# A two-layer hybrid attention kernel: the scores' product with the keys' low part on 128 rows

## The chip, the cores and the metric

The kernel runs on one core of one Trainium2 chip. The metric is the time of one execution on the device in microseconds (us); the kernel before takes 2376.73 us, the median of three runs (2375.67 to 2378.95). The rows below are from one more execution, taken by the hardware profiler. PE is TensorE's matmul, PEld its weight load, DVE is VectorE, ACT is ScalarE, POOL is GpSimd and SP is SyncE.

## The reference

Two layers work on 512 tokens of a sequence and 256 of a context, width 2048, all in float32. Layer 0 mixes pooling with latent attention of 12 heads; layer 1 mixes a matrix memory with attention of 16 heads in windows. Around both stand norms with an adaptive modulation, projections and a gate. Cut to the two attentions:

```python
def block_dense_attention(q, k, v):          # layer 0: head width 128 + 64 (rotated part)
    s = jnp.einsum('bqhd,bkhd->bhqk', qi, k).astype(F32) * scale
    p = jax.nn.softmax(s, axis=-1).astype(v.dtype)
    return jnp.einsum('bhqk,bkhd->bqhd', p, v)
...
def window_attention(q, k, v, kc, vc, sink): # layer 1: head width 64
    s_loc = jnp.einsum('bnqhgd,bnkhd->bnhgqk', qb, kb).astype(F32) * scale
    s_loc = jnp.where(mask[None, :, None, None], s_loc, -jnp.inf)
    s_ctx = jnp.einsum('bnqhgd,bchd->bnhgqc', qb, kc).astype(F32) * scale
    p = jax.nn.softmax(jnp.concatenate([s_loc, s_ctx, s_sink], axis=-1), axis=-1)
    ...
```

The rotated part of a latent head's keys is one vector of 64 numbers per token, shared by all 12 heads. In the window attention 8 query heads share one of two key heads of width 64. The sequence's queries see up to three blocks of 128 local keys and all 256 keys of the context.

## The kernel before

Every float32 operand of a matmul is held as two parts, a high part (rounded to the type float32r) and a low part, the rest. A product of two such operands is made of three: high by high, high by low, low by high. `split` (L108, L109) makes the parts: ACT copies the high part, DVE subtracts.

**A packed query.** Where the contraction is only 64 wide, the kernel puts both parts of a query into one tile of 128 rows: one half of the partitions holds the high part, the other half the low part (`qs` in the latent attention, L661 to 667; `wq` in the window attention, L1406 and L1407). Which half holds the high part depends on the head's parity. The keys stand twice, once on each half: KH and KL for the latent attention's rotated part (L432, L433, L480), KHw and KLw for the window attention (L1538 to L1552). One product of a packed query with KH gives high by high plus low by high. The third product, high by low, takes the half `hs` of the query's tile that holds the high part, and the same half of KL: 64 rows instead of 128.

**Latent attention** (650 to 1040 us). A unit is 256 queries of one head; there are 12 heads with three units each, and the third is the context's, which sees 256 keys instead of 768. `s_stage` (L669 to L693) computes the scores of 128 queries into a PSUM tile s: five products (three for the 128 wide part, then KH, then KL), each once over 512 keys and once over 256, or once over 256 alone in the third unit. DVE takes the maximum (L690), ACT the exponential (L691), DVE scales (L693). `t_stage` transposes the probabilities on PE (L708) and splits them, `o_stage` multiplies them with the values (L726). Between these parts PE works on the projections of later heads (L619, L639) and, for the last heads, on the out-projection (L776): `run(n)` issues a set number of columns of them. PE's order is the order of the program text (`manual_schedule`); the order on DVE and ACT is found by a scheduler, with `high_priority` for the softmax and the splits.

**Window attention** (1915 to 2245 us). `Softmax.heads` (L1452 and after) computes the scores of two heads for 128 queries. For each of the two heads it issues the KHw products with the local keys (L1461) and the context's (L1462). Then come the KLw products (L1466), for the local keys of the first and the second head, then for the context's keys of the first and the second head; the two heads of a pair use opposite halves of the partitions. There are 32 such calls; the outer two blocks of queries see 256 local keys, the inner two 384. DVE adds the mask and takes the maximum (L1470, shown as ISA or CUSTOM_DVE). `w_values` transposes a block of 128 keys' probabilities into wpt (L1583), splits it into wph and wpl, and multiplies with the values (L1593, L1594). In between, `run` issues products of the next projections and of the out-projection (L1419).

Of the kernel before, what the change touches and what calls it, by code (L numbers as in the profile page):

```python
# [9 lines left out]
F32R = mybir.dt.float32r  # L10
# [6 lines left out]
P = 128  # L17
# [11 lines left out]
# columns of the packed vector table  # L29
V_GB, V_SINK, V_PS, V_QN, V_KVN, V_HN, V_FN, V_NW, V_AB = 0, 16, 32, 36, 40, 44, 52, 68, 132  # L30
V_N = 132 + 192
# columns of the constant matrices
# [6 lines left out]
def tile_hybrid_dit(ctx: ExitStack, tc: tile.TileContext, ts: dict, out: bass.AP, dbg=None, upto=99):  # L39
# [6 lines left out]
    class Banks:  # L46
        """a PSUM pool: how many buffers each tag has; the buffers of pm can be taken out of their turn"""
# [16 lines left out]
    class Ring:  # L64
        """the buffers of one tag of a pool"""
# [45 lines left out]
    def load_w(src, n=1024, w=256, low=V):  # L111
        """-> for each block of 128 rows its (high, low) parts [128, w]"""
        raw = wp.tile([P, 1024], F32, name="wraw", tag="wraw", bufs=3)
        DM.dma_start(raw[:, :n], src)
        res = []
        m = n // 2
        for i in range(2):
            wh = wp.tile([P, 512], F32R, name="wh", tag="wh", bufs=4)
            wl = wp.tile([P, 512], F32R, name="wl", tag="wl", bufs=4)
            split(raw[:, i * m : (i + 1) * m], wh[:, :m], wl[:, :m], low)  # L120
            res += [(wh[:, k * w : (k + 1) * w], wl[:, k * w : (k + 1) * w]) for k in range(m // w)]
        return res

# [1 line left out]
    def ada_place(u, pb, n):  # L125
        """pb: [32, vectors, 16], column 32 b + c of the unit at [c, :, b]"""
# [7 lines left out]
    def ada_steps(u, pp, tp, nb=3, nt=2):  # L134
        """one unit of 512 columns on the tensor engine, in four steps"""
# [18 lines left out]
    def ada_vec_steps(u, pp, tp, nb, ttag, tbufs):  # L154
        """one unit of 512 columns on the vector engines: partial sums on every partition, then their sum"""
# [30 lines left out]
    class Background:  # L186
        """modulation units done step by step between other work; a unit's last product comes a few steps into the next one"""
# [30 lines left out]
    def rstd_col(ps6, nb, mul=None, bufs=2):  # L218
        """[128 tokens, nb] mean squares -> 1/rms"""
# [12 lines left out]
    def rows(v3, nb, pp, rb):  # L232
        """[128 tokens, nb] -> rb [128, nb*128], the same on every partition"""
# [24 lines left out]
    def h_chunk(j, xt, rb, u0, layer, hh, hl, tp, vs=(0, 1), low=V):  # L258
        """chunk j of the modulated rows; vs: 0 sequence, 1 context; rb, hh, hl: one AP for each"""
# [19 lines left out]
    def tmode(px, pc, w, kcs, Hx, Hc, first, last):  # L279
        """features on partitions; px/pc: one AP for each block of 128 columns; Hx/Hc: chunks (h, l)"""  # L280
# [12 lines left out]
    def kmode(ps, w, kcs, Hs, first, last, share):  # L293
        """tokens on partitions; ps: one AP for each block of 128 tokens; share: blocks in one bank"""
# [14 lines left out]
    def do_rope(ps, r, tmp):  # L309
        """ps [128, >=512] -> r[:, :512] rotated"""  # L310
# [11 lines left out]
    # =====================================================================  # L322
    # layer 0: pooling and latent attention
    # =====================================================================
    es0 = ExitStack()      # h
    esP = ExitStack()      # psum of the first phases
# [17 lines left out]
    # startup: statistics, modulation, h, and the first four blocks of columns  # L344
# [44 lines left out]
    def load_kr(q):  # L389
        """high and low parts of four chunks of the weights of k_r"""  # L390
# [6 lines left out]
    EARLY = 4           # units up to this one load beside the unused half of h  # L397
    PLAN = (0, 2, 3, 3, 2)      # blocks of columns done behind the steps of the next unit
# [43 lines left out]
    def c_evac(pairs, ssq):  # L442
        """raw latents and the sum of their squares"""
# [24 lines left out]
    # k_r of the context (its columns twice)  # L468
# [26 lines left out]
    # c_q  # L495
# [10 lines left out]
    # pooling  # L506
    m = NP - 16

    def pool_mean(g, px, pc):
        """difference between the windows' means and the values, split"""  # L510
# [57 lines left out]
    # a_gate  # L568
# [42 lines left out]
    # projections of the heads: generators that yield after every few products  # L611
# [57 lines left out]
    def s_stage(un, qi):  # L669
        """scores of 128 queries and their softmax"""  # L670
# [5 lines left out]
        hs = slice(64 * (head % 2), 64 * (head % 2) + 64)  # L676
        s = new_s2()
        qq = slice(u * 256 + qi * P, u * 256 + qi * P + P)
        prs = ((qh[:, qq], kh), (qh[:, qq], kl), (ql[:, qq], kh), (qs[:, qq], KH), (qs[hs, qq], KL[hs]))
# [68 lines left out]
    # the first group of the out-projection starts with the sequence's rows of the chunks that fit beside the last heads  # L748
# [3 lines left out]
    def zx_load(js):  # L752
        """sequence's part of two chunks"""
# [40 lines left out]
    def run(n):  # L794
        """n columns more"""
        state[0] += n
        while state[0] > 0:
            m = next(fill, None)
            if m is None:
                return  # L800
            state[0] -= m

    units = [(h, u) for h in range(12) for u in range(3)]
    FILL = ((3700, 4500, 4500), (3700, 4500, 4500), (2200, 2200, 2200))      # columns after each part of a unit
    SLOW = {(10, 0): 0.5, (10, 1): 0.5, (10, 2): 0.5, (11, 0): 0.3, (11, 1): 0.3, (11, 2): 1}      # what is left for the last two heads
    HEAD = 12 * NT      # columns of one projection of a head
# [59 lines left out]
    def zc_load(q):  # L866
        """context's part of four chunks"""
# [28 lines left out]
    def stats1(v):  # L896
        """1/rms of the sequence or of the context on every partition, in place of the sum"""
# [10 lines left out]
    # layer 1's rows of the sequence, while the context goes through  # L908
# [21 lines left out]
    # =====================================================================  # L930
    # layer 1: matrix memory and window attention
    # =====================================================================
# [31 lines left out]
    mm = opool(e2, "mm")          # what the matrix memory keeps  # L964
    C0 = [(mm.tile([P, 258], F32R, name=f"c0h{i}"), mm.tile([P, 258], F32R, name=f"c0l{i}")) for i in range(8)]
    emv = ExitStack()
    cm = opool(emv, "cmv")        # context only
    mkc = (cm.tile([P, 2, 512], F32R, name="mkch"), cm.tile([P, 2, 512], F32R, name="mkcl"))

    # v of head 0 with the gates  # L970
# [34 lines left out]
    # k  # L1005
# [13 lines left out]
    # gates  # L1019
# [16 lines left out]
    S.activation(g2, g1, AF.Exp, scale=-1.0)              # e = exp(-|f|)  # L1036
    V.tensor_scalar(g3, g2, 1.0, None, op0=ALU.add)       # y = 1 + e
    S.activation(g4, g3, AF.Ln)
    V.tensor_scalar(g1, g3, 1.0, None, op0=ALU.subtract)  # y - 1
    V.tensor_tensor(g1, g2, g1, op=ALU.subtract)          # what 1 + e lost  # L1040
    V.reciprocal(g2, g3)
    V.tensor_tensor(g1, g1, g2, op=ALU.mult)
    V.tensor_tensor(g4, g4, g1, op=ALU.add)               # log1p(e)
# [9 lines left out]
    # context: log weights of its positions in its final state  # L1053
    acol = gs.tile([P, 2, 2, 4], F32, name="acol")
    pa_ = pmt("pac", [P, 2, 2, 4])
    for d in range(2):
        far, near = (0, 1) if d == 0 else (1, 0)   # the far block also decays over the whole near one
# [27 lines left out]
    # sequence: local cumulative sums, block totals, running maxima  # L1085
# [18 lines left out]
    negM = [gp.tile([36, 4, P], F32R, name=f"negM{d}") for d in range(2)]   # high parts in rows 0-3, low ones in 32-35  # L1104
# [41 lines left out]
    # exp(-m_t), the inter-block offsets, the exponents' biases  # L1146
# [17 lines left out]
    # v of the other heads  # L1164
# [29 lines left out]
    # keys and values of the window attention  # L1194
# [178 lines left out]
    # first window group, while the last head goes through  # L1373
# [39 lines left out]
    def steps(px, w, kcs, bs, Hs, first, last):  # L1413
        """products of some chunks with some blocks of columns, one at a time"""
# [7 lines left out]
    def w_proj(i):  # L1422
        """queries and gates of a group"""
# [20 lines left out]
    class Softmax:  # L1444
        """scores of four heads for 128 queries and their softmax"""
# [6 lines left out]
        def heads(self, pair):  # L1452
# [7 lines left out]
            for a, s in zip(pair, ss_):  # L1460
                T.matmul(s[:, 512 - nl : 512], qs[i][a][:, qq], KHw[g][:, b0 * P : b1 * P], start=True, stop=False)  # L1461
                T.matmul(s[:, 512:768], qs[i][a][:, qq], KHw[g][:, NX:], start=True, stop=False)  # L1462
            for dst, ks in ((slice(512 - nl, 512), slice(b0 * P, b1 * P)), (slice(512, 768), slice(NX, NT))):
                for a, s in zip(pair, ss_):
                    hf = slice(64 * (a % 2), 64 * (a % 2) + 64)
                    T.matmul(s[:, dst], qs[i][a][hf, qq], KLw[g][hf, ks], start=False, stop=True)  # L1466
# [23 lines left out]
    def out_steps(g, px):  # L1490
        """all but the last two chunks"""
# [17 lines left out]
    def fillers():  # L1509
        """the other groups' projections, then the first three groups of the out-projection"""  # L1510
# [14 lines left out]
    PRE, PRE2, PRE3, RATE, RATE_END = 16, 8, 20, 9.5, 13      # products done ahead, and for each block of keys  # L1525
# [11 lines left out]
    # keys: rotated, split, each kv head on both halves of the partitions  # L1537
# [15 lines left out]
    vhl = ap2.tile([P, 6, 2, P], F32R, name="vhl")      # high and low parts side by side  # L1553
# [7 lines left out]
    # masks over the local blocks and the context  # L1561
# [12 lines left out]
    def w_values(i, nb, kc, prs, st_):  # L1574
        """one block of 128 keys: its part of what the four heads attend to, [features, queries] of their two blocks"""
# [259 lines left out]
```

## Time and profile before

| what | value |
|---|---|
| three timed runs, median (lowest, highest) | 2376.73 us (2375.67, 2378.95) |
| span of the profiled execution, first to last instruction | 2376.1 us |
[...]
| PE busy over the span | 2269.3 us |
| PEld busy | 1897.2 us |
| DVE busy | 1492.2 us |
| ACT busy | 1041.0 us |
| POOL busy | 462.4 us |

The profiled execution's own device time is not listed apart from its span; the median of the timed runs is 0.6 us above the span, which is what lies around the first and the last instruction. Busy time of PE is the union of its matmuls' durations. These overlap: the next matmul starts long before the one before it has ended, so the pace is read from the starts. A row of the timeline gives the start, the length, the engine, the line, the operation, what it writes and reads, the rows and columns of the array that it uses (128\*128, or 64\*128 for a product on half of the rows), its shape and how many like it follow one another directly; idle time of the engine just before it stands in brackets.

### The profile page before, as it was taken

The page shows a single profiled execution, that of the slowest core. Times are in us where ns is not written, and L with a number is a line of the kernel's source. Part 1 is how long each engine was busy: PE and PEld are TensorE (multiplying, and loading weights), DVE is VectorE, ACT ScalarE, POOL GpSimd, SP SyncE. Part 2 cuts the span into 40 slices and gives each one's busy share as a digit, 9 for nine tenths or more (in the row PEclk, how much of TensorE's full clock was granted, in tenths as well). Part 3 has the DMA queues.
Part 4 walks back from the last instruction along what each step waited for, and adds up shares of the span by engine and source line. Part 5 has one row for each costly group of instructions (what it writes and reads, how often), then busy time and mean ns, then how long its engine had stood idle before and what let it go on. Part 6 is the DMA issues. An engine that isn't in the chain of part 4 may idle for free.

```text
span 2376.1 us, 34745 instructions
## 1 busy us (share of the span) xinstructions
PE 2269.3 (96%) x12920; PEld 1897.2 (80%) x12920; DVE 1492.2 (63%) x2748; ACT 1041.0 (44%) x2054; POOL 462.4 (19%) x393
## 2 busy tenths in 40 slices
PE   5999998899999999999999999999999999998997
PEld 3678887788888888878888798998888877776886
DVE  5578888866466666668767822522555576778435
ACT  4234444443344444454224522222555556666333
POOL 0015575754100000016311200000000000003111
PEclk9999999999999999999999999999999999999998
DMA  9854454553211111255675322123222211113333
GB/s 384 312 195 160 169 186 155 186 200 137 81 47 58 47 52 54 70 169 206 227 246 190 136 100 80 56 79 112 98 97 96 102 58 65 60 63 116 133 120 138
DMA packets 118586, 311.27 MB, mean 131 GB/s; under 512 B 13676, under 2 KB 21356, under 8 KB 118416
## 3 DMA queue, kind: packets, MB, share of 16 engines
q1 hardware_dynamic: 111536, 281.73, 34.5%
q0 software_dynamic: 6880, 27.32, 3.0%
q8 instruction: 101, 1.65, 0.3%
q14 instruction: 69, 0.57, 0.1%
HBM read 279.37 MB, written 29.62 MB: 130 GB/s over the span
## 4 chain that ended last, share of the span: by engine, by line
PE 70%; DVE 8%; issue 3%; ACT 2%; DMA 2%; POOL 2%; SPq 0%; DVEq 0%; ACTq 0%; POOLq 0%
PE px L289 20%; PE px L302 11%; PE pj L619 6%; PE pc L291 5%; PE px L1419 5%; PE s L683 5%; PE pc L302 3%; PE om L726 3%; PE pj L639 2%; PE s L1419 2%; PE po L1338 2%; PE tp L708 2%; POOL acc L169 1%; DVE wl L109 1%; DMA at<-in_ada_dram 1%
## 5 line engine op out<-in xcount | busy, mean ns | idle before, releaser
L109 DVE TENSOR_TENSOR wl<-wraw,wh 128x512 fp32r<-128x512 f32 (+2 forms) x556 | 429.9, 780 | 422.9 <-ACT wh L108 414.8
L108 ACT CAST wh<-wraw 128x512 fp32r<-128x512 f32 (+2 forms) x556 | 324.4, 589 | 605.8 <-PE pc L291 137.3
L169 POOL TENSOR_TENSOR acc<-acc,at 128x512 f32<-128x512 f32 x180 | 285.1, 1584 | 282.6 <-ACT at L167 272.5
L164 DVE SCALAR_TENSOR_TENSOR acc<-at,st,acc 128x512 f32<-128x512 f32 x240 | 246.5, 1027 | 53.5 <-DMA at<-in_ada_dram 49.6
L167 ACT ACTIVATE at<-at,st 128x512 f32<-128x512 f32 x180 | 130.0, 724 | 180.8 <-DVE acc L164 157.2
L302 PE MATMUL px<-wh,hxh 128*128 128x512 f32 (+2 forms) x512 | 174.2, 340 | 0.2 <-ACT akx L1201 0.2
L302 PE MATMUL px<-wl,hxh 128*128 128x512 f32 (+2 forms) x512 | 173.7, 339 | 0.0
L302 PE MATMUL px<-wh,hxl 128*128 128x512 f32 (+2 forms) x512 | 173.6, 339 | 0.0
L289 PE MATMUL px<-h0h,wl 128*128 128x512 f32 x384 | 155.6, 405 | 10.4 <-DVE wl L109 10.3
L289 PE MATMUL px<-h0h,wh 128*128 128x512 f32 x384 | 155.9, 406 | 1.3 <-ACT wh L108 1.3
L289 PE MATMUL px<-h0l,wh 128*128 128x512 f32 x384 | 154.1, 401 | 0.0
L291 PE MATMUL pc<-h0l,wh 128*128 128x256 f32 x400 | 113.8, 285 | 0.0
L291 PE MATMUL pc<-h0h,wh 128*128 128x256 f32 x400 | 113.7, 284 | 0.0
L291 PE MATMUL pc<-h0h,wl 128*128 128x256 f32 x400 | 113.7, 284 | 0.0
L302 PEld LDWEIGHTS px<-wh,hxh 128*128 128x128 f32 x512 | 96.2, 188 | 12.9 <-ACT sz L1262 1.0
L302 PEld LDWEIGHTS px<-wl,hxh 128*128 128x128 f32 x512 | 96.2, 188 | 11.3
L302 PEld LDWEIGHTS px<-wh,hxl 128*128 128x128 f32 x512 | 96.2, 188 | 11.0
L289 PEld LDWEIGHTS px<-h0h,wl 128*128 128x128 f32 x384 | 73.5, 191 | 31.1 <-DVE wl L109 13.9
L289 PE MATMUL px<-zxh,wh 128*128 128x512 f32 x224 | 89.6, 400 | 2.5 <-DVE x L855 2.5
L289 PE MATMUL px<-zxh,wl 128*128 128x512 f32 x224 | 89.2, 398 | 2.5 <-DVE wl L109 2.4
L289 PEld LDWEIGHTS px<-h0h,wh 128*128 128x128 f32 x384 | 73.6, 192 | 20.1 <-ACT wh L108 2.6
L289 PE MATMUL px<-zxl,wh 128*128 128x512 f32 x224 | 89.6, 400 | 0.0
(875 smaller groups left out, 6209.9 us busy)
## 6 DMA issues: line engine op xcount, KB each, us to landing
at<-in_ada_dram SPq DMA_DIRECT2D x256, 256.0 KB, 2.9
at<-in_ada_dram SPq DMA_DIRECT2D x64, 512.0 KB, 8.0
wraw<-in_od_in_dram SPq DMA_DIRECT2D x64, 512.0 KB, 3.4
wraw<-in_ev_in_dram SPq DMA_DIRECT2D x56, 512.0 KB, 4.2
wraw<-in_ev_out_dram SPq DMA_DIRECT2D x44, 512.0 KB, 4.2
wraw<-in_od_out_dram SPq DMA_DIRECT2D x36, 512.0 KB, 3.4
wraw<-in_od_oz_dram SPq DMA_DIRECT2D x32, 512.0 KB, 3.4
xt<-in_xT_dram SPq DMA_DIRECT2D x16, 384.0 KB, 7.5
```

Source lines behind the costliest of these rows:

```text
L108: S.copy(h, src)
L109: low.tensor_tensor(l, src, h, op=ALU.subtract)
L164: V.scalar_tensor_tensor(acc[0], at, st[:, kc, 0:1], acc[0], op0=ALU.mult, op1=ALU.add)
L167: S.mul(m, at, st[:, kc, 1:2])
L169: G.tensor_tensor(acc[1], acc[1], m, op=ALU.add)
L289: T.matmul(px[b], w_, Hx[kc][r_], start=s0, stop=s1)
L291: T.matmul(pc[b], w_, Hc[kc][r_], start=s0 and b == 0, stop=s1, skip_group_check=True)
L302: T.matmul(p_, h_, w_, start=s0, stop=s1, skip_group_check=True)
L619: T.matmul(t, w_, r_[:, sl], start=kc == 0 and n == 0, stop=kc == 3 and n == 2)
L683: T.matmul(s[:, c0 - k0 : c1 - k0], l_, r_[:, c0:c1], start=n == 0, stop=n == 4)
L726: T.matmul(o[:, :256], v_[:, 6 - nk + b, :], p_[:, b, :], start=b == 0 and n == 0, stop=b == nk - 1 and n == 2)
L1419: T.matmul(px[b], w_, Hs[kc][r_], start=first and i == 0 and n == 0, stop=last and i == len(kcs) - 1 and n == 2)
```

## The change

In `s_stage` the KL product takes the whole packed query and the whole of KL, 128 rows. The slice `hs` goes. In `Softmax.heads` the KLw products take 128 rows too, and the order of the products changes: all four products of the first head (KHw local, KHw context, KLw local, KLw context), then the four of the second. The sums gain the product low by low, which was left out before. The changed file also drops comments and docstrings, so its line numbers are up to three lower; nothing else is changed.

```diff
     def s_stage(un, qi):
...
-        hs = slice(64 * (head % 2), 64 * (head % 2) + 64)
         s = new_s2()
         qq = slice(u * 256 + qi * P, u * 256 + qi * P + P)
-        prs = ((qh[:, qq], kh), (qh[:, qq], kl), (ql[:, qq], kh), (qs[:, qq], KH), (qs[hs, qq], KL[hs]))
+        prs = ((qh[:, qq], kh), (qh[:, qq], kl), (ql[:, qq], kh), (qs[:, qq], KH), (qs[:, qq], KL))
         for n, (l_, r_) in enumerate(prs):
             for c0 in range(k0, NT, 512):
...
             for a, s in zip(pair, ss_):
-                T.matmul(s[:, 512 - nl : 512], qs[i][a][:, qq], KHw[g][:, b0 * P : b1 * P], start=True, stop=False)
-                T.matmul(s[:, 512:768], qs[i][a][:, qq], KHw[g][:, NX:], start=True, stop=False)
-            for dst, ks in ((slice(512 - nl, 512), slice(b0 * P, b1 * P)), (slice(512, 768), slice(NX, NT))):
-                for a, s in zip(pair, ss_):
-                    hf = slice(64 * (a % 2), 64 * (a % 2) + 64)
-                    T.matmul(s[:, dst], qs[i][a][hf, qq], KLw[g][hf, ks], start=False, stop=True)
+                q = qs[i][a][:, qq]
+                for n, K in enumerate((KHw[g], KLw[g])):
+                    T.matmul(s[:, 512 - nl : 512], q, K[:, b0 * P : b1 * P], start=n == 0, stop=n == 1)
+                    T.matmul(s[:, 512:768], q, K[:, NX:], start=n == 0, stop=n == 1)
```

In the latent attention PE's order stays as it is, and so do DVE's and ACT's. In the window attention PE's order changes within each call. The first place is the call for heads 2 and 3 of the second block of queries, on PE, before (s_19210 and s_19211 are the two heads' score tiles, KHw_18980 and KLw_18982 the keys' parts, wq the packed queries):

```order
L1461 MATMUL s_19210<-KHw_18980,wq 128x384
L1462 MATMUL s_19210<-KHw_18980,wq 128x256
L1461 MATMUL s_19211<-KHw_18980,wq 128x384
L1462 MATMUL s_19211<-KHw_18980,wq 128x256
L1466 MATMUL s_19210<-KLw_18982,wq 128x384
L1466 MATMUL s_19211<-KLw_18982,wq 128x384
L1466 MATMUL s_19210<-KLw_18982,wq 128x256
L1466 MATMUL s_19211<-KLw_18982,wq 128x256
```

The same call on PE in the changed kernel:

```order
L1462 MATMUL s_19210<-KHw_18980,wq 128x384
L1463 MATMUL s_19210<-KHw_18980,wq 128x256
L1462 MATMUL s_19210<-KLw_18982,wq 128x384
L1463 MATMUL s_19210<-KLw_18982,wq 128x256
L1462 MATMUL s_19211<-KHw_18980,wq 128x384
L1463 MATMUL s_19211<-KHw_18980,wq 128x256
L1462 MATMUL s_19211<-KLw_18982,wq 128x384
L1463 MATMUL s_19211<-KLw_18982,wq 128x256
```

The first head's tile is complete after the fourth product, where before it was complete after the seventh; the second head's is complete after the eighth in both.

The scheduler orders DVE's queue anew in the window attention. The second place is DVE's queue for the same two heads, before (the ISA rows on wpr are the masked maximum of one head each, wpl the low part of a block of transposed probabilities, wmx the row maxima):

```order
L1470 ISA wpr__19220,wm_19221<-s_19210,msk 128x640
L1470 ISA wm_19221 128x1
L109 TENSOR_TENSOR wpl<-wpt,wph 128x512
L1471 SCALAR_TENSOR_TENSOR wmx<-wm_19221,nsink 128x1
L1470 ISA wpr__19225,wm_19226<-s_19211,msk 128x640
L1470 ISA wm_19226 128x1
```

And DVE's queue there in the changed kernel:

```order
L1467 ISA wpr__19220,wm_19221<-s_19210,msk 128x640
L1467 ISA wm_19221 128x1
L1467 ISA wpr__19225,wm_19226<-s_19211,msk 128x640
L1467 ISA wm_19226 128x1
L109 TENSOR_TENSOR wpl<-wpt,wph 128x512
L1468 SCALAR_TENSOR_TENSOR wmx<-wm_19221,nsink 128x1
```

The low part wpl has moved behind the second head's masked maximum. Of the 72 wpl instructions, nine stand behind one masked maximum more than before, and none stands behind fewer. ACT's queue is moved in the same places; POOL's and SP's are the same.

## Rows read from the trace of the kernel before

**Rows 1.** The page's first part: busy time of an engine in us, its share of the span, and its instructions.
```profile
PE 2269.3 (96%) x12920; PEld 1897.2 (80%) x12920; DVE 1492.2 (63%) x2748; ACT 1041.0 (44%) x2054; POOL 462.4 (19%) x393
```

**Rows 2.** The chain of waits in the stretch from 650 to 1040 us, its shares by line.
```profile
by line: PE pj L619 31.6%; PE s L683 28.4%; PE om L726 15.1%; PE pj L639 11.9%; PE tp L708 9.2%; PE pj L776 2.3%; DVE ptl L109 0.4%; DVE qnl L109 0.2%; ACT pth L108 0.2%; ACT pr L691 0.1%; ACT zxh L108 0.1%; ACT wh L108 0.1%; issue 0.1%; AC
```

**Rows 3.** Busy time by stretch: from and to, length, then PE, PEld, DVE, ACT and POOL with their instructions, the granted clock, the share and rate of the DMA engines.
```profile
650.00:1040.00 390.00, 387.46 (x2464) 330.84 (x2463) 257.24 (x548) 178.28 (x426) 12.65 (x16) 1.00 0.18 61
1915.00:2245.00 330.00, 313.58 (x1563) 243.61 (x1562) 230.23 (x536) 203.09 (x390) 34.52 (x29) 0.99 0.24 81
```

**Rows 4.** What PE waited for from 650 to 1040 us: line, who ended the wait, us in total, times, longest.
```profile
PE pj L776 <- ACT zxh L108: 1.0, 1, 1.0
PE pj L619 <- DVE qnl L109: 0.7, 1, 0.7
PE pj L639 <- ACT qrr L659: 0.6, 1, 0.6
```

**Rows 5.** The matmuls of L683 with KH and with KL: count, lowest, median and highest length in ns, first and last start in us, shapes with their counts.
```profile
L683 PE MATMUL s<-KH,qs x120: 274/280/399, 655.4 to 1037.1; 128*128 128x256 f32 x72, 128*128 128x512 f32 x48
...
L683 PE MATMUL s<-KL,qs x120: 275/381/500, 655.8 to 1037.3; 64*128 64x256 f32 x72, 64*128 64x512 f32 x48
```

**Rows 6.** The timeline of PE around a score stage with 768 keys, where each row marked x2 is a product of 512 and one of 256 columns.
```profile
700.51 0.51 PE L683 MATMUL s<-knl,qnh 128*128 128x512 f32 x2
700.86 0.53 PE L683 MATMUL s<-knh,qnl 128*128 128x512 f32 x2
701.22 0.50 PE L683 MATMUL s<-KH,qs 128*128 128x512 f32 x2
701.66 0.61 PE L683 MATMUL s<-KL,qs 64*128 64x512 f32 x2
702.20 0.39 PE L639 MATMUL pj<-wh,ckvh 128*128 128x256 f32 x1
702.42 0.28 PE L639 MATMUL pj<-wl,ckvh 128*128 128x256 f32 x1
702.54 0.29 PE L639 MATMUL pj<-wh,ckvl 128*128 128x256 f32 x1
```

**Rows 7.** The same around a score stage with 256 keys.
```profile
709.65 0.28 PE L683 MATMUL s<-KH,qs 128*128 128x256 f32 x1
709.86 0.38 PE L683 MATMUL s<-KL,qs 64*128 64x256 f32 x1
710.17 0.39 PE L639 MATMUL pj<-wh,ckvl 128*128 128x256 f32 x1
710.39 0.28 PE L639 MATMUL pj<-wh,ckvh 128*128 128x256 f32 x1
710.51 0.29 PE L639 MATMUL pj<-wl,ckvh 128*128 128x256 f32 x1
```

**Rows 8.** The weight loads of the stage of rows 6.
```profile
701.66 0.29 PEld L683 LDWEIGHTS s<-KL,qs 64*128 64x128 f32 x2 [0.24 <-issue]
702.20 0.19 PEld L639 LDWEIGHTS pj<-wh,ckvh 128*128 128x128 f32 x1 [0.25 <-issue]
702.31 0.19 PEld L639 LDWEIGHTS pj<-wl,ckvh 128*128 128x128 f32 x1
```

**Rows 9.** The 64-row products of the window attention, in the columns of rows 5.
```profile
L1466 PE MATMUL s<-KLw,wq x128: 271/372/579, 1924.2 to 2187.3; 64*128 64x256 f32 x96, 64*128 64x384 f32 x32
```

**Rows 10.** The timeline of PE around a call with 256 local keys in the window attention; L1466 is the four 64-row products.
```profile
1927.03 0.28 PE L1461 MATMUL s<-KHw,wq 128*128 128x256 f32 x1
1927.15 0.28 PE L1462 MATMUL s<-KHw,wq 128*128 128x256 f32 x1
...
1927.38 0.28 PE L1462 MATMUL s<-KHw,wq 128*128 128x256 f32 x1
1927.60 0.50 PE L1466 MATMUL s<-KLw,wq 64*128 64x256 f32 x4
1928.03 0.50 PE L1419 MATMUL px<-hxh,wh 128*128 128x512 f32 x1
1928.37 0.39 PE L1419 MATMUL px<-hxl,wh 128*128 128x512 f32 x1
1928.60 0.39 PE L1419 MATMUL px<-hxh,wl 128*128 128x512 f32 x1
```

**Rows 11.** The same around a call with 384 local keys, from the second head's first product on, and the product that takes up wpl.
```profile
1938.99 0.34 PE L1461 MATMUL s<-KHw,wq 128*128 128x384 f32 x1
1939.17 0.28 PE L1462 MATMUL s<-KHw,wq 128*128 128x256 f32 x1
...
1939.87 0.51 PE L1419 MATMUL px<-hxh,wl 128*128 128x512 f32 x1
1940.21 0.40 PE L1419 MATMUL px<-hxh,wh 128*128 128x512 f32 x1
...
1942.55 0.39 PE L1594 MATMUL wpo<-wpl,vhl 128*64 128x512 f32 x1
```

**Rows 12.** The timeline of DVE at that place.
```profile
1940.72 0.69 DVE L109 TENSOR_TENSOR wpl<-wpt,wph 128x512 fp32r<-128x512 f32 x1
...
1941.39 0.82 DVE L1470 CUSTOM_DVE_ANT_0 wpr__19225<-s,msk 128x640 f32<-128x640 f32 x1
```

**Rows 13.** What L1594 on PE waited for from 1915 to 2245 us, in the columns of rows 4.
```profile
PE wpo L1594 <- DVE wpl L109: 3.4, 3, 1.6
```

## Prediction

> **What bounds the kernel now.** I read the page's busy times first: PE works 2269.3 of 2376.1 us, so what shortens the time must shorten PE's queue [rows 1]. Then the chain of waits over the latent attention (650 to 1040 us): nearly every piece of it is a PE line, 28.4% the scores at L683, 31.6% the head projections at L619; DVE and ACT pieces are under half a per cent each [rows 2]. [...] PE's waits for other engines add up to 2.3 us there [rows 4]. A microsecond less in PE's queue is therefore nearly a microsecond less in this stage. The window attention (1915 to 2245 us) is looser: PE 313.58 of 330.00 us, clock 0.99, DVE 230.23 and ACT 203.09 [rows 3].
>
> "Busy" hides something in these stages, because a matmul's row lasts longer than the time until the next one starts. So I go by starts. In the narrow units of the latent attention a 256-column product starts 0.12 us after the one before it [rows 7]; in the wide ones a 512-column and a 256-column product together take 0.35 to 0.36 us from pair to pair [rows 6]. That step breaks in one place only: around the product with KL, the one that uses 64 rows.
>
> **The change, part by part.** Nothing is added to PE's count of instructions and no column is added: 64 rows become 128, and the columns that pass through stay 512, 384 or 256. Three terms follow.
>
> *Latent attention, wide units.* There are 120 such products, 48 of 512 columns and 72 of 256 [rows 5]; so 48 stages issue two and 24 stages issue one. In a wide stage the first KH product starts at 701.22, the first KL product at 701.66 (0.44 later, where the pairs before came 0.35 and 0.36 apart), the next full-row product at 702.20, and the one after that at 702.42, still 0.22 behind it; only from 702.42 to 702.54 is the step 0.12 again [rows 6]. The weight loads tell why: the load for KL starts 0.24 us after the load before it has ended, in the same moment as its matmul, and the next full-row load is again 0.25 us late; the load after that starts at 702.31, while the matmul of 702.20 runs, as loads do elsewhere [rows 8]. [...] From 701.22 to 702.42 are 1.20 us. In step it would be two pairs of 0.355 and one 0.12, 0.83. That saves 0.37 us, times 48: **17.8 us**.
>
> *Narrow units.* From the KH product at 709.65 to the second product behind the KL one, 710.39, are 0.74 us [rows 7]; three steps of 0.12 make 0.36. That saves 0.38, times 24: **9.1 us**. This assumes that a 128-row product of the same columns goes in the step of the KH product; the row of the KH products has the same forms and counts as KL's [rows 5].
>
> *Window attention.* Here 32 calls each issue four 64-row products, half of the calls with 384 local keys and half with 256 [rows 9]. Two heads use opposite halves of the array, so their products stand side by side, and this is given up. In the call with 256 local keys, the stretch from the first KH product, 1927.03, to the second product behind the call, 1928.37, is 1.34 us [rows 10]. In full rows it is eight steps of 0.12 and one 512-column step of 0.23 (1928.37 to 1928.60), 1.19. That saves 0.15, times 16: 2.4 us. With 384 local keys the third KH product stands at 1938.99 and the second product behind the call at 1940.21, 1.22 us [rows 11]; in full rows 0.18 and 0.12 for the two KH products, twice 0.18 and twice 0.12 for the low parts, and 0.23, 1.13. That saves 0.09, times 16: 1.4 us. So the side-by-side products pay less than the two passages cost, if barely: **3.8 us** gained.
>
> *The order of the four products.* A head's scores are complete after four products instead of seven or eight, so DVE's masked maximum for the first head can begin about half a microsecond earlier. The scheduler has put DVE's and ACT's queues in another order for that. In nine of 72 places the low part wpl of a block of keys now stands behind one mask instruction more, and the PE product that needs it (L1594) waits behind it, with the whole of PE's queue. Price: the mask instruction takes 0.82 us. In the place shown, wpl runs 1940.72 to 1941.41 and PE takes it up at 1942.55 [rows 11, 12]; 1.14 us lie between, which cover 0.82. From below, the 3.4 us that PE now waits for wpl [rows 13] may vanish; from above, nine places without cover are 7.4 us. I take 0, since the shown place is covered.
>
> *What is late next.* With 26.9 us less PE time, the latent stage leaves the same DVE work (257.24 us) in 363 us, 71%. DVE's and ACT's evacuations of pj and tp then come due earlier. PE waits three times for such work now, 2.3 us in all [rows 4]. I let that double and give 2.3 us back; none is the lower end, half of the gain (13.5 us) the upper, a rival below.
>
> [...] The row shows four 64-row products of 256 columns begun within 1927.60 to 1928.03, 0.43 us, against 0.47 for four full-row steps of 0.12 [rows 10]. [...]
>
> *Sum.* 17.8 + 9.1 + 3.8 - 2.3 = 28.4 us. The profiled span is 2376.1 us; the median of three runs is 2376.73, so 0.6 us lie around the span. 2376.1 - 28.4 + 0.6 = **2348.3 us**.
>
> **Rivals.**
> 1. *Softmax and evacuation take over.* In the latent stage PE catches up with DVE and half of the 26.9 us returns as waits: 11.2 us more than I gave back, 2359.5 us. For it: DVE's share there rises to 71%, and DVE has many short jobs in a fixed order. Against it: of 72 stages only three waits show now [rows 4].
> 2. *The new order in the window attention.* Nine times 0.82 us uncovered: 2348.3 + 7.4 = 2355.7 us. For it: PE already waits 3.4 us for wpl there [rows 13]. Against it: the 1.14 us of cover in the place shown [rows 11, 12].
> 3. *Side by side was worth two.* The low products serially are 0.47 us in the 256 calls and 0.60 in the 384 calls; half of that, 0.24 and 0.30, lost 16 times each, is 8.6 us lost in place of 3.8 gained: 2348.3 + 12.4 = 2360.7 us. [...] Against it: the 0.43 us measured start to start, and the late start of the product behind [rows 10].
> 4. *The gaps stay.* What holds the KL product up is something other than its 64 rows (its place last in the accumulation, or the tile KL itself). Then nothing moves: 2376.7 us. Against it: in the window attention the 64-row products of another tile begin late as well (1927.38 to 1927.60, 0.22 us, where the step is 0.12), and KH, with the same stationary qs, is in step [rows 7, 10].
> 5. *Slower: the weight load is no longer hidden at all.* A 128-row KL product sits on the rows that the KH product before it uses; if its load (0.19 us [rows 8]) had to wait for that product, each of 120 + 128 products [rows 5, 9] would stand 0.19 us longer, 47.1 us: 2348.3 + 47.1 = 2395.4 us. It decides from 28.4 / 248 = 0.115 us per product on. Against it: the full-row load at 702.31 begins while the full-row matmul of 702.20, 0.39 us long, is under way [rows 6, 8]. [...]
>
> **How the numbers follow.** Forecast 0.75, rival 1 0.10, rival 2 0.07, rival 3 0.03, rival 4 0.03, rival 5 0.02. A measurement of this kernel can tell about 0.2%, 4.8 us, from no change. Faster by more than that are the forecast and rivals 1 to 3, 0.95; rival 4 is the same, 0.03; rival 5 slower, 0.02. The forecast's own spread: nothing given back and PE's waits for wpl gone, 2348.3 - 2.3 - 3.4 = 2342.6; at the other end rival 2 with a little more, 2357. I leave rivals 1, 3, 4 and 5 outside, 0.18: the range is 2342 to 2357 us.
>
> **What would show it.** In the changed kernel's trace the KL weight loads must start under the KH matmuls, with no idle time before them; the 0.22 us step behind the scores must be 0.12; a wide score stage must take five pairs of 0.35; the stretch of the latent scores (KL's first to last start is 655.8 to 1037.3 now [rows 5]) must be some 25 us shorter. In the window attention the four low products of a call must come 0.12 or 0.18 apart, one after another. Rival 1 shows as new PE waits for pj, pth or qnl in the latent stage; rival 2 as PE waits for wpl at the nine places; rival 5 as KL loads that start only when the KH matmul is done. I am wrong if the latent stage shrinks by less than 20 us, or if it shrinks and the layers behind it do not end earlier by as much.

## The result and the profile after

The changed kernel takes 2343.71 us, the median of four runs (2342.60 to 2345.14), beside 2377.35 us for the kernel before in the same comparison: a ratio of 0.9861 with a 95% interval of 0.9847 to 0.9874, 33.6 us less. A second comparison later gave 2341.17 us and 0.9849 (0.9836 to 0.9862). The forecast was 2348.3 us, the range 2342 to 2357; the first median lies inside it near its lower end, the second 0.8 us below it. The profiled span went from 2376.1 to 2343.4 us. Line numbers are up to three lower than before: the latent scores are L682 now, the window scores L1462 and L1463.

First, the page's busy times, to set against [rows 1]:

```profile
PE 2238.1 (96%) x12920; PEld 1902.8 (81%) x12920; DVE 1488.9 (64%) x2748; ACT 1041.4 (44%) x2054; POOL 459.0 (20%) x393
```

PE has the same 12920 instructions and 31.2 us less busy time; no other engine moved by more than 6 us. Where it went shows by stretch. These two stretches hold the work of the two in [rows 3], in the same columns:

```profile
650.00:1014.00 364.00, 360.50 (x2464) 329.20 (x2463) 254.15 (x548) 178.70 (x426) 12.78 (x16) 1.00 0.20 65
1890.00:2212.00 322.00, 307.00 (x1559) 248.04 (x1558) 228.90 (x536) 202.57 (x389) 34.62 (x29) 0.99 0.25 83
```

The latent stage needs 364 us for what took 390, at the same granted clock of 1.00; the window stage 322 us for 330. The rows that answer to [rows 5] fix the first number more closely:

```profile
L682 PE MATMUL s<-KL,qs x120: 278/282/403, 656.1 to 1011.3; 128*128 128x256 f32 x72, 128*128 128x512 f32 x48
...
  DVE nm L689: 14.6, 20
```

From the first KL product to the last are 355.2 us, where they were 381.5: 26.3 us less. The median length of one fell from 381 to 282 ns; KH's is 283. DVE's maximum waited for the scores 20 times, 14.6 us; in the kernel before it was 30 times, 22.7 us.

The timeline of PE in a wide score stage, as in [rows 6]:

```profile
693.95 0.52 PE L682 MATMUL s<-KH,qs 128*128 128x512 f32 x2
694.30 0.51 PE L682 MATMUL s<-KL,qs 128*128 128x512 f32 x2
694.65 0.28 PE L639 MATMUL pj<-wh,ckvh 128*128 128x256 f32 x1
694.77 0.28 PE L639 MATMUL pj<-wl,ckvh 128*128 128x256 f32 x1
```

The pairs come 0.35 us apart without a break, and the product behind the scores follows after 0.12. From the KH pair to the second product behind the scores are 0.82 us, where [rows 6] had 1.20. The weight loads there, as in [rows 8]:

```profile
694.19 0.31 PEld L682 LDWEIGHTS s<-KL,qs 128*128 128x128 f32 x2
694.54 0.19 PEld L639 LDWEIGHTS pj<-wh,ckvh 128*128 128x128 f32 x1
```

No load has a bracket: the KL loads end at 694.50, the next load begins 0.04 us later. Each begins while a matmul of the row before is under way: the KL load at 694.19, 0.11 us ahead of its own matmul, under the KH pair.

What PE waits for in the latent stage, 650 to 1014 us, beside [rows 4]:

```profile
PE pj L775 <- ACT zxh L108: 1.0, 1, 1.0
PE pj L619 <- DVE qnl L109: 0.9, 2, 0.7
PE pj L639 <- ACT qrr L659: 0.7, 1, 0.7
PE om L725 <- DVE ptl L109: 0.5, 1, 0.5
PE tp L707 <- DVE pr L692: 0.2, 1, 0.2
```

Two small waits are new, and the sum is 3.3 us, 1.0 more than before.

In the window attention, the timeline of PE in a call with 256 local keys, as in [rows 10]:

```profile
1902.07 0.29 PE L1462 MATMUL s<-KHw,wq 128*128 128x256 f32 x1
...
1902.31 0.28 PE L1462 MATMUL s<-KLw,wq 128*128 128x256 f32 x1
...
1903.02 0.40 PE L1418 MATMUL px<-hxh,wh 128*128 128x512 f32 x1
1903.26 0.39 PE L1418 MATMUL px<-hxl,wh 128*128 128x512 f32 x1
```

The eight products begin 0.12 us apart, and from the first to the second product behind the call are 1.19 us, for 1.34 before. The whole stage, from the first KHw product to the last, first before and then after:

```profile
L1461 PE MATMUL s<-KHw,wq x64: 277/364/562, 1923.0 to 2186.7; 128*128 128x256 f32 x32, 128*128 128x384 f32 x32
```

```profile
L1462 PE MATMUL s<-KHw,wq x64: 277/364/562, 1898.5 to 2154.2; 128*128 128x256 f32 x32, 128*128 128x384 f32 x32
```

263.7 us became 255.7, 8.0 less. The two stages together account for 34.3 us. Between them 1.5 us of the latent gain were lost in this execution: the last latent score came 26.0 us earlier, the first window score 24.5. In the profile of the second comparison almost nothing was lost there (27.7 and 27.5). So the gain needs no third place.

PE's waits in the window stage, 1890 to 2212 us:

```profile
PE wpo L1591 <- DVE wpl L109: 4.6, 6, 1.3
...
PE s L1462 <- DVE wm L1467: 0.2, 1, 0.2
```

The wait for wpl rose from 3.4 us in 3 places [rows 13] to 4.6 in 6. Two other waits of the kernel before went or shrank. Its view of the same waits has them:

```profile
PE px L1419 <- DVE wl L109: 2.4, 2, 1.5
...
PE s L1461 <- DVE wm L1470: 1.0, 3, 0.5
```

The wait for wl (the low part of a projection's weights) is gone from the view after, and that for wm (the row maximum, which frees the scores' tile) is 0.2. Over the whole view, the waits went from 16.3 us to 15.0. The view also holds a wait for ACT's az ahead of the first KHw product, 3.5 us before and 4.3 after; with only the latent attention changed it is 4.1 (the edit alone, below) and 4.3 (the version with 96 rows), so it moves without any change to this attention. From the first KHw product to the last the waits went from 12.8 us to 10.7.

### The profile page after: what moved, and what is told of

The parts are those of the page before. It is cut to its first block, busy times and chain, and to the rows that moved or that the text cites. A ratio compares the mean times of both kernels' runs of the same rounds, so it can differ in the third digit from the quotient of the medians.

```text
span 2343.4 us, 34744 instructions
## 1 busy us (share of the span) xinstructions
PE 2238.1 (96%) x12920; PEld 1902.8 (81%) x12920; DVE 1488.9 (64%) x2748; ACT 1041.4 (44%) x2054; POOL 459.0 (20%) x393
## 4 chain that ended last, share of the span: by engine, by line
PE 68%; DVE 9%; issue 4%; DMA 3%; POOL 2%; ACT 2%; DVEq 0%; SPq 0%; ACTq 0%; POOLq 0%
PE px L289 20%; PE px L302 11%; PE pj L619 5%; PE pc L291 5%; PE px L1418 5%; PE s L682 4%; PE pc L302 3%; PE om L725 3%; PE pj L639 2%; POOL acc L169 2%; DMA at<-in_ada_dram 2%; PE s L1418 2%; DVE acc L164 2%; PE po L1337 2%; DVE wl L109 2%
## 5 line engine op out<-in xcount | busy, mean ns | idle before, releaser
L289 PE MATMUL px<-h0h,wl 128*128 128x512 f32 x384 | 155.3, 404 | 11.7 <-DVE wl L109 11.7
L302 PEld LDWEIGHTS px<-wh,hxh 128*128 128x128 f32 x512 | 96.2, 188 | 12.8 <-ACT sz L1261 1.0
L289 PE MATMUL px<-hxl,wh 128*128 128x512 f32 x224 | 89.2, 398 | 0.0
```

Of the source, the lines that this page charges most:

```text
L289: T.matmul(px[b], w_, Hx[kc][r_], start=s0, stop=s1)
L302: T.matmul(p_, h_, w_, start=s0, stop=s1, skip_group_check=True)
```

## The experiments

The theory on trial: a passage from 128-row to 64-row work and back costs PE some 0.37 us, whatever the product does, and the change gains by taking passages out. Its rivals: something about the KL product itself (its tile, its place as the last of five); the number of rows as such; and, for the window attention, the new order and not the rows.

### The change in parts

**Latent attention alone** (the kernel before with the first edit only):

```diff
-        prs = (..., (qs[:, qq], KH), (qs[hs, qq], KL[hs]))
+        prs = (..., (qs[:, qq], KH), (qs[:, qq], KL))
```

> Only the latent attention's KL product goes on 128 rows; the window attention is as before. Theory (each passage between 64-row and 128-row work costs a gap): 72 stages lose 0.37 to 0.38 us each, 26.9 us less waits that come in their place, so 24 to 27 us faster than before, about 2351 us. Rival (much of the gain is the new order in the window attention): less than 18 us faster.

Measured: 2351.7 us, ratio 0.9895 (0.9883 to 0.9908), 24.4 us less than the 2376.14 us of the kernel before in the same comparison. Its row for the KL products:

```profile
L683 PE MATMUL s<-KL,qs x120: 278/281/402, 654.4 to 1009.7; 128*128 128x256 f32 x72, 128*128 128x512 f32 x48
```

355.3 us from first to last, 26.2 less than before and within 0.1 of the full change. This one edit makes the latent gain.

**Window attention alone** (rows and order, as in the change):

> Only the window attention is changed (128 rows and the new order); the latent attention is as before. Theory: 3.8 us from the rows, and what the traces of before and after differ by from the first to the last score there, 8.0 us, at most: 4 to 8 us faster than before. Rival (two heads side by side are worth more than the gaps): slower than before by 4 us or more.

Measured: 2367.61 us, 0.9964 (0.9952 to 0.9976), 8.5 us less by the medians, just above the 4 to 8 that were expected. The stage, as in the rows above:

```profile
L1463 PE MATMUL s<-KHw,wq x64: 277/364/562, 1921.6 to 2178.8; 128*128 128x256 f32 x32, 128*128 128x384 f32 x32
```

From the first KHw product to the last are 257.2 us, 6.5 less than before.

**The window's rows alone**, in the old order of products:

```diff
-                    T.matmul(s[:, dst], qs[i][a][hf, qq], KLw[g][hf, ks], start=False, stop=True)
+                    T.matmul(s[:, dst], qs[i][a][:, qq], KLw[g][:, ks], start=False, stop=True)
```

> Only the window attention's KLw products go on 128 rows, in the order of before (two heads in turn). Theory (the rows give 3.8 us, the order the other 4): 3 to 5 us faster than before and 3 to 5 us slower than with the new order. Rival (the order gives nothing and the rest was chance of waits): as with the new order within 1.5 us.

Measured: 2374.84 us over twelve runs that scatter from 2369.42 to 2379.53, 0.9995 (0.9986 to 1.0004). By time alone this is no change, where 3 to 5 us were expected. Against the rows with the new order it is slower by time too: that interval, 0.9952 to 0.9976, lies wholly below this one, and the medians are 7.2 us apart. How much of this the order makes is read from the traces, which are finer:

```profile
L1461 PE MATMUL s<-KHw,wq x64: 278/364/562, 1918.9 to 2179.6; 128*128 128x256 f32 x32, 128*128 128x384 f32 x32
```

That is 260.7 us, 3.0 less than before and 3.5 more than with the order. The stretch repeats well. In the five traces whose window attention is as before it is 263.6 to 264.2 us; in the two with the rows and the old order 260.7 both times; in the five with rows and new order 255.7 to 257.2. Two of the waits here:

```profile
PE px L1419 <- DVE wl L109: 2.3, 2, 1.4
...
PE s L1461 <- DVE wm L1469: 1.1, 3, 0.5
```

These stand as in the kernel before. When the order is changed too, the wait for wl is gone and that for wm is 0.2 us. From the first KHw product to the last all waits are 13.7 us here and 10.5 with rows and order: the 3.2 us between them are most of the 3.5 us of the stretch. In the kernel before they are 12.8. The rows alone thus raised the waits by 0.9 us, and PE's products by themselves gained 3.0 + 0.9 = 3.9 us.

**Both attentions on 128 rows, old order:**

> Both attentions on 128 rows, the window attention in the order of before. Theory as for the window alone: 3 to 5 us slower than the changed kernel, about 2348 us. Rival (the order is worth nothing): 2342 to 2346 us, as the changed kernel.

Measured: 2346.58 us, 0.9871 (0.9857 to 0.9884), 2.9 and 5.4 us more than the two medians of the changed kernel; KHw's first to last is 260.7 us again. Beside it the changed kernel's 0.9861 and 0.9849 lie lower, but the intervals overlap; by the times of this pair the order's share isn't settled. By the traces it is 260.7 - 255.7 = 5.0 us here and 3.5 in the pair above. Part of the 5.0 us is the clock. Over this stretch the mean granted clock is 0.98 here and 1.00 in the changed kernel. In the kernel before, it is 0.50 from 1921.30 to 1924.70 us, and a 512-column product there, begun at 1921.47, takes 0.43 us to the next start at 1921.90. Such starts stand in two places here, where eight products of 512 columns take 0.42 to 0.43 us, in place of 0.23; one of them, with the next starting at 2128.44:

```profile
2128.02 0.63 PE L1419 MATMUL px<-z1h,wh 128*128 128x512 f32 x1
```

The changed kernel has none between its first and its last KHw product, so this makes at least 1.5 of the 5.0 us. The waits, 12.5 us here and 10.7 in the changed kernel, make 1.8. By its waits the order is worth 2 to 3 us.

**The window's order alone**, on 64 rows:

```diff
-            for a, s in zip(pair, ss_):
-                ... two KHw products; then, for all heads, the KLw products on hf
+                hf = slice(64 * (a % 2), 64 * (a % 2) + 64)
+                for n, (r, K) in enumerate(((slice(0, P), KHw[g]), (hf, KLw[g]))):
+                    q = qs[i][a][r, qq]
+                    T.matmul(s[:, 512 - nl : 512], q, K[r, b0 * P : b1 * P], start=n == 0, stop=n == 1)
+                    T.matmul(s[:, 512:768], q, K[r, NX:], start=n == 0, stop=n == 1)
```

> The window attention in the new order, but the low products still on 64 rows, so that a head's two 64-row products stand alone between full-row ones; the latent attention is as before. Theory (a price per passage): four passages in a call in place of two, and no two heads side by side; per call two gaps of 0.37 to 0.38 us on the full-row pace, 1.19 + 0.76 = 1.95 us in place of 1.34 with 256 local keys, 1.43 + 0.76 = 2.19 in place of 1.52 with 384: about 20 us slower than before, 2395 to 2399 us. Rival (the order alone gives the gain in this attention): 2 to 8 us faster than before.

Measured: 2391.03 us, 1.0056 (1.0034 to 1.0078), 13.2 us slower than 2377.79 and short of the 20 that were expected. The same call as in [rows 10], on PE:

```profile
1924.69 0.28 PE L1464 MATMUL s<-KHw,wq 128*128 128x256 f32 x1
...
1925.01 0.38 PE L1464 MATMUL s<-KLw,wq 64*128 64x256 f32 x1
1925.24 0.28 PE L1465 MATMUL s<-KLw,wq 64*128 64x256 f32 x1
...
1926.64 0.40 PE L1419 MATMUL px<-hxl,wh 128*128 128x512 f32 x1
```

The call has two pairs of passages instead of one and takes 1.95 us to the second product behind it, for 1.34 before. Note the two rows with KLw: on one head's half the two 64-row products do not stand side by side, they come 0.23 us apart. The stage grew from 263.7 to 277.8 us, 14.1, less than the calls' sum of some 20, since PE waits less: 10.9 us, 5.4 less than before. No wait for wl or wm is left. Whether the order took them away here, or PE's slower pace, this run can't tell. So the order that costs most with 64 rows costs nothing with 128.

### The theory itself

**More passages.** In the 48 wide stages the first KL product is put ahead of the KH pair, so that the two 64-row products no longer share one passage:

```diff
+        seq = [(n, c0) for n in range(5) for c0 in range(k0, NT, 512)]
+        if k0 == 0:
+            seq.remove((4, 0))
+            seq.insert(6, (4, 0))
```

> Latent attention, still 64 rows; in the 48 stages with 768 keys the KL product of 512 columns is moved away from the one of 256, behind the third product's 512 columns, so that full-row products stand between the two. The same work, twice the passages in these stages. Theory (a price per passage): 48 more gaps of 0.37 us, 17.8 us slower than before, 2393 to 2397 us. Rival (64-row products are slow by themselves, or what is last in the sum): as before within 3 us.

Measured: 2398.24 us, 1.0084 (1.0066 to 1.0102), 20.5 us slower than 2377.79 and just above the range expected. A wide stage on PE:

```profile
696.56 0.52 PE L688 MATMUL s<-knh,qnl 128*128 128x512 f32 x2
697.01 0.49 PE L688 MATMUL s<-KL,qs 64*128 64x512 f32 x1
697.43 0.62 PE L688 MATMUL s<-KH,qs 128*128 128x512 f32 x2
697.98 0.38 PE L688 MATMUL s<-KL,qs 64*128 64x256 f32 x1
698.29 0.39 PE L619 MATMUL pj<-cql,wh 128*128 128x256 f32 x1
698.51 0.28 PE L619 MATMUL pj<-cqh,wl 128*128 128x256 f32 x1
```

From 696.56 to 698.51 are 1.95 us, where the step would give three pairs of 0.355 and one 0.12, 1.18. The 0.77 us too much are two passages of 0.385. Neither columns nor instructions were added: 48 times 0.385 is 18.5 us, and the latent scores' stretch (by knh's first and last start) grew by 401.4 - 382.3 = 19.1.

**The other product on 64 rows.** KH takes the half, KL the whole:

```diff
-        prs = (..., (qs[:, qq], KH), (qs[hs, qq], KL[hs]))
+        prs = (..., (qs[hs, qq], KH[hs]), (qs[:, qq], KL))
```

> Latent attention: KL on 128 rows, KH on 64 (the rotated query's low part by the keys' high part is left out). Theory (the number of rows makes the gap, not the tile or the place): the gap moves to the KH product, the passages are as many: as before within 3 us. Rival (the tile KL or the last place in the sum makes the gap): 20 to 27 us faster than before.

Measured: 2378.44 us, 1.0007 (0.9997 to 1.0017). A narrow stage, beside [rows 7]:

```profile
709.66 0.29 PE L683 MATMUL s<-knh,qnl 128*128 128x256 f32 x1
709.87 0.38 PE L683 MATMUL s<-KH,qs 64*128 64x256 f32 x1
710.19 0.38 PE L683 MATMUL s<-KL,qs 128*128 128x256 f32 x1
710.41 0.28 PE L639 MATMUL pj<-wh,ckvl 128*128 128x256 f32 x1
```

KH is late now, 0.21 us, and KL behind it, which has 128 rows, another 0.32 in place of 0.12. The gap goes with the rows, not with the tile KL and not with the last place.

**How many rows.** The even heads' KL product takes rows 0 to 95, the odd heads' the 64 rows as before:

```diff
-        hs = slice(64 * (head % 2), 64 * (head % 2) + 64)
+        hs = slice(0, 96) if head % 2 == 0 else slice(64, 128)
```

> Latent attention: for the heads whose own half is the lower one (half of the 72 stages) the KL product takes 96 rows, their 64 and 32 of the other half (a part of low by low comes into the sum); the other heads stay on 64 rows. If the gap comes with a passage between a half array and a full one only: half of the gain, 13 us faster than before, 2362 to 2366 us. If any number of rows below 128 costs it: as before within 3 us.

Measured: 2363.06 us, 0.9935 (0.9915 to 0.9956), 14.7 us less. Its row for KL:

```profile
L683 PE MATMUL s<-KL,qs x120: 276/332/499, 656.9 to 1025.0; 96*128 96x256 f32 x36, 64*128 64x256 f32 x36, 96*128 96x512 f32 x24, 64*128 64x512 f32 x24
```

A wide stage with 96 rows on PE:

```profile
656.94 0.51 PE L683 MATMUL s<-KL,qs 96*128 96x512 f32 x2
657.29 0.39 PE L619 MATMUL pj<-cqh,wl 128*128 128x512 f32 x1
```

The KL pair takes its 0.35 us to the next start. The row gives 368.1 us, 13.4 less than before: half of the change's 26.3, from the half of the heads that went to 96 rows. In the kernel before, KL's weight loads follow idle time in 48 places, 11.7 us; here in 24, 5.8 us. A product on 96 rows is in step; the cost does not fall with the rows bit by bit.

### Other passages in the program

The changed kernel still has products on 36 rows (selh, in the matrix memory) and on 4 rows. Padded with zeros to 128 rows they should be in step too. **The 36-row products:**

```diff
-    selh = lp.tile([36, 4, P], F32R, name="selh")
-    S.copy(selh.rearrange("p h t -> p (h t)"), selr[0:36])
+    selh = lp.tile([P, 4, P], F32R, name="selh")
+    G.memset(selh.bitcast(F32), 0.0)
+    S.copy(selh[0:36].rearrange("p h t -> p (h t)"), selr[0:36])
```

> The changed kernel, and the matrix memory's eight 36-row products (four groups of two, line 1288 of the changed kernel) padded with rows of zeros to 128. In the changed kernel's trace the stretch from the full-row product before such a group to the second one behind it is 1.32 us (1649.52 to 1650.84) where four steps of 0.233 make 0.93. Theory (any work on fewer rows than 64 pays the same passages): 0.39 us less in each of the four stretches, 1.6 us in all, which the trace shows and the time hardly can. Rival (36 rows are something else): the stretch stays at 1.32 us.

Measured: 2345.97 us, 0.9869 (0.9853 to 0.9885), beside 2341.17 us, 0.9849 (0.9836 to 0.9862), for the changed kernel in the same comparison: 4.8 us more by the medians, with intervals that overlap. One of the four places in the changed kernel, then padded:

```profile
1649.52 0.40 PE L302 MATMUL px<-wh,hxl 128*128 128x512 f32 x1
1649.85 0.73 PE L1288 MATMUL bc<-negM,selh 36*128 36x512 f32 x2
...
1650.84 0.40 PE L1308 MATMUL sc<-mql,mkh 128*128 128x512 f32 x1
```

```profile
1646.11 0.39 PE L302 MATMUL px<-wh,hxl 128*128 128x512 f32 x1
1646.34 0.62 PE L1289 MATMUL bc<-negM,selh 128*128 128x512 f32 x2
...
1647.03 0.39 PE L1309 MATMUL sc<-mql,mkh 128*128 128x512 f32 x1
```

1.32 us became 0.92, the 0.40 that the theory says, at each place. Four times that is 1.6 us, and the time does not show it.

**The 4-row products as well** (the tiles wr, dg4 and M filled up with zeros by POOL, their transposes written as products):

> As the one before, and the matrix memory's 16 products on 4 rows, in eight groups, padded to 128 rows too: no work on 64 rows or fewer is left in the program. Theory: about 0.3 us less at each of the eight further places, 4 us less than the changed kernel in all, 2339 to 2341 us against 2343.7. Rival (PE waits there for DVE's short steps anyway, or the added clearing of tiles on POOL delays them): no less, or slower.

A miss: 2343.57 us, 0.9857 (0.9844 to 0.9871), no better than the changed kernel. Padding helped at some places and hurt at others. Around one transpose of M, from the full-row product before it to the second one behind, 0.59 us became 0.45. Around four that follow one another 0.77 became 1.14: on PE the four are four instructions on 4 rows before, and eight on 128 rows once they are padded products. So this version changed more than the rows, and the passages of the 4-row products have no price of their own here. None of the versions beat the changed kernel by what can be measured.

## Why the prediction was right, point by point

The forecast was 28.4 us of gain; the profiled spans give 32.7. Of the 4.3 us between them the latent attention makes 1.7 and the window attention 4.2; 1.6 were lost outside the two stretches.

- *Wide and narrow units, 26.9 us.* Right, step and size. The 1.20 us of a wide stage became 0.82 (0.83 was forecast). The latent stretch lost 26.3 us net in the full change and 26.2 in the edit alone; with the 1.0 us of added waits the direct gain is 27.3. What the gap consists of is less sure than its size. The rows show the 64-row load starting with its matmul, both at 701.66 [rows 6, 8], where the 128-row load now starts 0.11 us ahead; why it starts late was not shown.
- *Given back, 2.3 us.* The mechanism was right and the size was off: PE's waits there grew by 1.0 us, not by 2.3. Rival 1 (the softmax takes over) put 13.5 us there and is refuted. DVE's maximum waits less for the scores than before, 14.6 us in place of 22.7, but it still waits; DVE follows PE.
- *Window rows, 3.8 us.* Right by the trace: 3.9 us with the old order. The 256 call came out as forecast to the hundredth (1.19 us). The times of the rows alone don't show it. The stage loses 8.0 us in all. The rows make 3.9 of it and the waits 2.1; the other 2.0 are not taken apart. Some of it is the clock, 0.99 before and 1.00 after over the stretch.
- *The order of the four products, 0.* This is the term that failed. It was taken as 0, with a gain of 3.4 us at most from wpl. The traces show a gain of 2 to 3 us by the waits (3.2 and 1.8 us in the two pairs), and it comes from elsewhere. From the kernel before to the changed one the wait for wl, 2.4 us, goes, that for wm falls from 1.0 to 0.2, and the wait for wpl rises by 1.2 us. The prediction looked only at the nine moved wpl and their cover, not at the other work in the same queues that would come earlier.
- *The range.* Its lower end, 2342.6 us, was set for nothing given back and no wait for wpl. The measured 2343.71 us lies close to it for other reasons, so that it lies there is luck. The 0.6 us put around the span is too little as well: the changed kernel's profiled execution took 2345.14 us with a span of 2343.4, 1.7 us more, and with that the same sum forecasts 2349.4.
- *Rival 2 (the nine wpl uncovered, 7.4 us).* Refuted: 1.2 us more. DVE's queue at the place shown in the prediction, after:

```profile
1913.91 0.82 DVE L1467 CUSTOM_DVE_ANT_0 wpr__19225<-s,msk 128x640 f32<-128x640 f32 x1
1914.66 0.69 DVE L109 TENSOR_TENSOR wpl<-wpt,wph 128x512 fp32r<-128x512 f32 x1
```

wpl is done at 1915.35 and PE takes it up at 1916.09: it stands behind the second head's mask now, and 0.74 us of cover are left.
- *Rival 3 (side by side worth two, 2360.7 us).* Refuted by the rows-only kernel: serial products on 128 rows are not slower than four side by side with their two passages. The gap, in and out, measures 0.37 to 0.40 us here. The two-fold gain that the rival supposes does not come about with four products between two passages: side by side, two of them begun within 0.01 us at 1927.60, the 256 call took 1.34 us, one after another 1.19.
- *Rival 4 (the gaps stay).* Refuted by the latent edit alone; its reasons, tile and place, by the swap.
- *Rival 5 (loads no longer hidden, 47 us lost).* Refuted: the KL loads start 0.11 us ahead of their own matmul, under the KH pair on the same 128 rows.

Open: which part of the reordering removed the waits for wl and wm. PE finishes the first head's scores earlier, and the scheduler writes DVE's and ACT's queues in another order; both came with one edit, and no run here holds one fixed. Open too is why the medians with the old and the new order on the window alone are 7.2 us apart when the stretch differs by 3.5: the two profiled executions differ by only 1.0 us in their spans.

## What to carry to other kernels

Where PE sets the pace, count the passages between products on 64 rows and products on 128, not the rows: each way in and out cost some 0.37 us here (0.40 with 36 rows), three steps of a 256-column product, and rows that are filled up cost nothing in the two attentions (a 256-column KL or KLw product on 128 rows takes the 0.12 us of its neighbours), as long as what they add to the sum may be there. Four products of 256 columns side by side between two passages did not pay here, 1.34 us a call beside 1.19; whether more of them would was not shown. When an edit lets a result be complete earlier, look at all that waits in the queues behind it, since the scheduler's new order may give something of its own: 2 to 3 us here, next to the 3.9 of the rows.

## What was not expected of the hardware

- 96 rows are in step (the KL pair takes 0.35 us to the next start) and 64 are not (0.54 [rows 6]), and it isn't the size of the operand: a product with 64 *columns* of the array in use (wpl's, 128\*64) begins 0.22 us behind a 512-column product and the next 0.24 us behind it, which is the plain step (0.23 us in [rows 10]).

```profile
1915.87 0.39 PE L1590 MATMUL wpo<-wph,vhl 128*128 128x512 f32 x1
1916.09 0.40 PE L1591 MATMUL wpo<-wpl,vhl 128*64 128x512 f32 x1
1916.33 0.27 PE L1580 MATMUL wpt<-con,wpr__19069 128*128 128x128 f32 x1
```

- The price of a passage hardly depends on what passes: 0.385 us on average where a product of 512 and one of 256 columns on 64 rows stand alone, 0.37 and 0.38 in the wide and narrow stages before, 0.40 with two products on 36 rows.
